# A list scheduler's model of the chip: side products kept in runs, PSUM banks counted whole, later loads

## The chip, the cores and the metric

The kernel runs on one NeuronCore of a Trainium2 chip. The metric is the device time of one execution in microseconds (us); smaller is better. TensorE is PE in the profile (its weight loads are PEld), VectorE is DVE, ScalarE is ACT, GpSimd is POOL, and SyncE is SP, which issues almost all transfers.

## What is computed

One inference step of a four-layer trunk on 384 tokens (128 context, 256 latent) of width 2048, in float32 from end to end. Each layer does

```
x += gate * W_out( mixer(RMSNorm(x) * (1 + scale) + shift) * silu(z) )
(shift, scale, gate) = silu(cond) @ W_ada_l + b_ada_l
```

Layers 0 and 3 mix by windowed attention (16 heads, 4 key heads), layer 1 by neighbourhood attention (16 heads), layer 2 by a gated MLP with normed spatial mixing. Weights of about 580 MB are read once.

## The kernel before

Every big product is made exact enough by splitting both operands into a high and a low part (`H`, `L` for a weight unit, `hH`, `hL` for the activations) and adding three fp32r products: high by high, high by low, low by high. A weight unit is 128x1024 (512 KB). SP loads it into one of four `raw` buffers, ACT copies it to `H`, DVE subtracts to get `L`, and PE multiplies: 24 products of 384 columns ("A" form: the output has 384 tokens) or 18 of 512 columns ("B" form, 3 token blocks). These are 13,824 **main products**, and all of them read `hH` or `hL`. The rest on PE are **side products**: transposes (of queries, keys and softmax rows, by `ident`), scores (`qT` against keys, and a mask added through `identR`), probabilities times values (`PTH`, `PLT`), the small condition products (`sT`, `spad`, four column tiles each), `sel`, `ones` and the mixing products of layer 2 (`aux`).

DVE also makes two thirds of the condition products by itself: it takes a transposed weight tile `araw` (512 KB, two buffers, loaded by SP) and the broadcast condition `cbc`, and reduces their product, twice for each tile (lines named `junk<-araw,cbc`). When such a pass goes from one half of the condition to the other, `cbc` is loaded again from `srow`.

The score group of one head (`head`) writes two PSUM banks, `b0` and `b1`: the context block and the first latent block go to `b0`, the second to `b1`. DVE then takes row maxima of these banks (`vmax`, in the trace `sm<-bk`).

What sets the order: the program first records all operations in the order of its Python code (class `Rec`, method `add`) and then emits them in an order of its own. `add` notes for each operation which earlier ones it needs: `data` (it waits until they are done) or `order` (same engine, it only follows). Main products are chained to each other and keep their order (`self.main`). Ranges within a tile are told apart in grains of 8 columns (`span`), so for a PSUM bank a read of the first 128 columns does not touch a write of the others. `cost` gives each operation a duration and a latency, `in_order` makes a first timetable, `due` the latest time by which each operation is wanted, and `schedule` is a list scheduler: the engine that can start first takes its ready operation with the smallest key (PE: the number in the program; others: the due time). Three passes of `due` and `schedule` follow each other (`order`). `schedule` before has a rule for PE: an operation under 100 ns (`long` is false) is held back in favour of one over 100 ns while a weight load (`LDW`, 108 ns apart, `LAG` 56 ns before the product) would not be finished. A transfer counts as landed 1300 ns after its turn in the queue.

The emitted order is fixed for each engine; the waits between engines are put in when the program is built, and those on a PSUM bank hold for the bank's users as they then stand in the order.

Of the kernel before, what the change touches and what calls it, by code (L numbers as in the profile page):

```python
# [10 lines left out]
F32R = mybir.dt.float32r  # L11
# [38 lines left out]
class Rec:  # L50
# [9 lines left out]
    def __init__(self, nc):  # L60
        self.real, self.ops, self.bytes = nc, [], {}
        for e in ("tensor", "vector", "scalar", "gpsimd", "sync"):
            setattr(self, e, _Eng(self, e))
        self.wr, self.rd, self.bank, self.tiles, self.main = {}, {}, {}, {}, None

    @staticmethod
    def span(ap):

        if not hasattr(ap, "tensor"):
            ap = ap[:, :]  # L70
        name = re.match(r"[A-Za-z]+\d*", ap.tensor.name).group()
        p = [[int(v) for v in x] for x in ap.ap]
        if name in ("i", "o"):
            return None
        if name in ("xs", "srow"):
            return name, 0, 8, name
        lo = int(ap.offset) % max(p[0][0], 1)
        hi = lo + sum(s * (n - 1) for s, n in p[1:] if s > 0) + 1
        return name, lo, hi, ap.tensor.name
# [8 lines left out]
    def cost(self, e, op, a, k):  # L88

        n = self.cols(a[0] if a else k["out"])  # L90
        if e == "tensor":
            if op == "transpose":
                d = 57
            elif "tile_position" in k:
                d = 128
            elif a[2].dtype == F32R:
                d = (n + 32) / 2.4 if n > P else 57
            else:
                d = max(4 * (n + 16) / 2.4, 224)
            return d, d + 190  # L100
        if e == "vector":
            if op == "tensor_tensor_reduce":
                return n / 0.96 + 250, n / 0.96 + 330
            if op in ("tensor_tensor", "tensor_copy", "bn_stats", "tensor_reduce"):
                m = self.cols(k.get("in_", a[1] if len(a) > 1 else None)) if op == "tensor_reduce" else 512 if op == "bn_stats" else n
                d = m / 0.96 + 72
            elif op == "scalar_tensor_tensor":
                d = n / 0.96 + (129 if hasattr(k["scalar"], "ap") else 70)
            elif op == "tensor_scalar":
                d = n / 1.92 + 190  # L110
            else:
                d = n / 0.96 + 90
            return d, d + 90
        if e == "scalar":
            if op == "dma_start":
                return 400, 2600
            d = n / 1.2 + 97 + (75 if hasattr(k.get("scale"), "ap") or hasattr(k.get("bias"), "ap") else 0)
            d += 95 if "accum_out" in k else 0
            return d, d + 115
        if e == "gpsimd":  # L120
            return 650 + 140 * n, 750 + 140 * n
        return 330, 2100
# [7 lines left out]
    def add(self, e, op, a, k):  # L130
        i = len(self.ops)
        w = [k[x] for x in self.OUTS if x in k] + ([a[0]] if a else [])
        r = [v for x, v in k.items() if x not in self.OUTS] + list(a[1:])
        w = [self.span(x) for x in w]
        r = [self.span(x) for x in r if hasattr(x, "ap") or hasattr(x, "tensor")]
        data, order = set(), set()
        G = self.GRAIN
        for s in r + w:
            if s:
                t = self.tiles.get(s[0])  # L140
                if t is None or t[0] != s[3]:
                    for x in t[1] if t else ():
                        (order if self.ops[x][0] == e else data).add(x)
                    self.tiles[s[0]] = s[3], [i]
                elif t[1][-1] != i:
                    order.add(t[1][0])
                    t[1].append(i)
        for s in r:
            if s:
                for g in range(s[1] // G, (s[2] - 1) // G + 1):  # L150
                    x = self.wr.get((s[0], g))
                    if x is not None:
                        data.add(x)
        for s in w:
            if s:
                for g in range(s[1] // G, (s[2] - 1) // G + 1):
                    x = self.wr.get((s[0], g))
                    if x is not None:
                        (order if self.ops[x][0] == e == "tensor" else data).add(x)
                    for x in self.rd.get((s[0], g), ()):  # L160
                        (order if self.ops[x][0] == e else data).add(x)
                if s[0][:2] == "bk" and e == "tensor":
                    x = self.bank.get(s[0])
                    if x is not None:
                        order.add(x)
                    self.bank[s[0]] = i
        if e == "tensor" and any(s and s[0] in ("hH", "hL") for s in r):
            if self.main is not None:
                order.add(self.main)
            self.main = i  # L170
        self.ops.append((e, op, a, k))
        for s in r:
            if s:
                for g in range(s[1] // G, (s[2] - 1) // G + 1):
                    self.rd.setdefault((s[0], g), []).append(i)
        for s in w:
            if s:
                for g in range(s[1] // G, (s[2] - 1) // G + 1):
                    self.wr[s[0], g] = i
                    self.rd[s[0], g] = []  # L180
        if not hasattr(self, "dep"):
            self.dep, self.dur, self.lat, self.eng, self.load, self.long = [], [], [], [], [], []
        order -= data
        self.dep.append([(x, True) for x in data] + [(x, False) for x in order])
        d, l = self.cost(e, op, a, k)
        self.dur.append(d)
        self.lat.append(l)
        self.eng.append("tensor vector scalar gpsimd sync".split().index(e))
        self.long.append(d > 100)
        self.load.append(self.dma_bytes(a) / 395.0 if op == "dma_start" else 0)  # L190

    SEM, LDW, LAG = 45, 108, 56

    def ready_at(self, i, start, done, margin=0):
        t, e = 0.0, self.eng[i]
# [5 lines left out]
                t = v  # L201
        return t

    def in_order(self):

        n = len(self.ops)
        free, dma = [0.0] * 5, 0.0
        start, done = [0.0] * n, [0.0] * n
        load = last = 0.0
        for i in range(n):  # L210
            e = self.eng[i]
            t = max(free[e], self.ready_at(i, start, done))
            if e == 0:
                load = max(load + self.LDW, last)
                t = last = max(t, load + self.LAG)
            start[i] = t
            free[e] = t + self.dur[i]
            if self.load[i]:
                dma = max(dma, t + 700) + self.load[i]
                done[i] = max(dma + 1300, t + self.lat[i])  # L220
            else:
                done[i] = t + self.lat[i]
        return start, done
# [13 lines left out]

    MARGIN = 250

    def schedule(self, late):  # L240
        n = len(self.ops)
        succ, left = [[] for _ in range(n)], [0] * n
        for i in range(n):
# [1 line left out]
            for x, _ in self.dep[i]:  # L245
                succ[x].append(i)
        start, done = [0.0] * n, [0.0] * n
        free, dma, load = [0.0] * 5, 0.0, 0.0
        wait, ready = [[] for _ in range(5)], [[] for _ in range(5)]
        key = [float(i) if self.eng[i] == 0 else late[i] for i in range(n)]  # L250
        for i in range(n):
            if not left[i]:
                heapq.heappush(wait[self.eng[i]], (0.0, i))
        count, last = 0, 0.0
        while count < n:
            best, be = None, None
            for e in range(5):
                if ready[e]:
                    t = free[e]
                    if e == 0 and not any(self.long[i] for _, i in ready[0]):  # L260
                        t = max(t, load + self.LDW + self.LAG)
                elif wait[e]:
                    t = max(free[e], wait[e][0][0])
                else:
# [5 lines left out]
                i = heapq.heappop(wait[e])[1]  # L270
                heapq.heappush(ready[e], (key[i], i))
            i = ready[e][0][1]
            if e == 0:
                if load + self.LDW + self.LAG > t and not self.long[i]:
                    i = min((i for _, i in ready[0] if self.long[i]), default=i)
                if i != ready[0][0][1]:
                    ready[0].remove((key[i], i))
                    heapq.heapify(ready[0])
                    heapq.heappush(ready[0], (-1.0, i))
                load = max(load + self.LDW, last)  # L280
                t = last = max(t, load + self.LAG)
            if e in (1, 2) and wait[e]:
                end, hold = t + self.dur[i], None
                for est, j in wait[e]:
# [7 lines left out]
            free[e] = t + self.dur[i]  # L292
            if self.load[i]:
                dma = max(dma, t + 700) + self.load[i]
                done[i] = max(dma + 1300, t + self.lat[i])
            else:
                done[i] = t + self.lat[i]
            count += 1
# [4 lines left out]
        return start, done  # L303

    def order(self, passes=3):
        start, done = self.in_order()
        for _ in range(passes):
            start, done = self.schedule(self.due(start))
# [1461 lines left out]
```

## Time and profile before

| what | value |
|---|---|
| three runs | 3052.76, 3053.60, 3056.09 us (median 3053.6) |
| the profiled execution | 3048.99 us, of which the span from first to last instruction is 3047.2 |
| PE busy | 3005.5 us (99%), 17,064 products |
| PE weight loads busy | 2733.9 us (90%) |
| DVE busy | 2085.1 us (68%) |
| ACT busy | 1202.4 us (39%) |
| DMA | 598.95 MB, mean 197 GB/s |
| mean granted PE clock | 0.998 |

PE's busy time counts products that overlap as one; a product is shown from its start to the end of its pipeline, so 384 columns show 0.33 us though the next one starts 0.17 us later. What a product costs is therefore read from start to start. Idle time in brackets in a timeline is the engine's, with the operation that ended it.

Stages by the trace: layer 0 to 645 us (its startup to about 180), layer 1 to 1405, layer 2 from 1405 to 2508 (its first products, for the mixing input, to about 1680), then layer 3.

### The profile page before, as it was taken

The numbers are of one execution on the slowest core, as the hardware profiler recorded it, in microseconds if no ns is written. First come the engines' busy times: TensorE is split into PE (matmuls) and PEld (weight loads), VectorE is DVE, ScalarE is ACT, GpSimd is POOL, SyncE is SP. The second block draws the span as 40 slices with busy tenths as digits, with TensorE's granted clock in tenths as the row PEclk, the third lists the DMA queues.
The fourth block names the chain that finished last, engine by engine and source line by source line (L and its number), as shares of the span: only waits on it lengthen the run. The fifth ranks groups of instructions, "written<-read, shape, count | busy, mean of one in ns | idle before, by whom it ended". The sixth has DMA issues, their size and how long they took to land.

```text
span 3047.2 us, 44052 instructions
## 1 busy us (share of the span) xinstructions
PE 3005.5 (99%) x17064; PEld 2733.9 (90%) x17064; DVE 2085.1 (68%) x3499; ACT 1202.4 (39%) x2175; POOL 59.0 (2%) x29
## 2 busy tenths in 40 slices
PE   8999999999999999999999999999999999999999
PEld 4788899988888888998878999999999998888999
DVE  4568798669898988899898974334355556444554
ACT  3344445353444444534223222222233235354542
POOL 0000000000000000000000000000000000000000
PEclk9999999999999999999999999999999999999999
DMA  9857667767676777788788663444454454333433
GB/s 384 327 164 233 206 194 250 265 212 232 210 230 211 230 214 254 249 271 275 255 261 261 200 194 123 126 126 123 128 159 138 143 188 135 121 98 104 135 108 125
DMA packets 187354, 598.95 MB, mean 197 GB/s; under 512 B 21764, under 2 KB 47620, under 8 KB 187140
## 3 DMA queue, kind: packets, MB, share of 16 engines
q1 hardware_dynamic: 186712, 596.00, 60.4%
q8 instruction: 133, 2.18, 0.3%
q14 instruction: 77, 0.63, 0.1%
q10 hardware_dynamic: 432, 0.13, 0.0%
HBM read 580.31 MB, written 15.75 MB: 196 GB/s over the span
## 4 chain that ended last, share of the span: by engine, by line
PE 87%; DVE 5%; DMA 5%; issue 2%; ACT 1%; SPq 0%; DVEq 0%; ACTq 0%
PE bk L314 87%; DMA araw<-i_w_adaT 3%; DVE junk L314 2%; DVE L L314 2%; DMA raw<-i_win_B 0%; DVE pair L314 0%; DMA cbc<-srow 0%; DVE bn L314 0%; DMA pair<-i_xT 0%; DVE sm L314 0%; ACT Pt L314 0%; DVE Pt L314 0%; ACT H L314 0%; DMA pair<-i_masks 0%; DMA sel<-i_sel 0%
## 5 line engine op out<-in xcount | busy, mean ns | idle before, releaser
L314 ACT ACTIVATE H<-raw 128x1024 fp32r<-128x1024 f32 x640 | 678.2, 1060 | 1498.8 <-PE bk L314 1378.4
L314 DVE TENSOR_TENSOR L<-raw,H 128x1024 fp32r<-128x1024 f32 x640 | 782.4, 1223 | 447.3 <-ACT H L314 445.6
L314 PE MATMUL bk<-hH,H 128*128 128x384 f32 x3072 | 1040.4, 339 | 3.6 <-DVE pair L314 3.6
L314 PE MATMUL bk<-hL,H 128*128 128x384 f32 x3072 | 1034.0, 337 | 0.0
L314 PE MATMUL bk<-hH,L 128*128 128x384 f32 x3072 | 1031.5, 336 | 0.7 <-DVE L L314 0.7
L314 PE MATMUL bk<-H,hH 128*128 128x512 f32 x1536 | 607.7, 396 | 5.7 <-ACT hH L314 3.8
L314 PE MATMUL bk<-L,hH 128*128 128x512 f32 x1536 | 605.4, 394 | 1.4 <-DVE L L314 1.2
L314 PE MATMUL bk<-H,hL 128*128 128x512 f32 x1536 | 601.9, 392 | 0.0
L314 PEld LDWEIGHTS bk<-hH,H 128*128 128x128 f32 x3072 | 578.1, 188 | 14.1 <-DVE pair L314 5.0
L314 PEld LDWEIGHTS bk<-hH,L 128*128 128x128 f32 x3072 | 577.7, 188 | 1.5 <-DVE L L314 1.0
L314 PEld LDWEIGHTS bk<-hL,H 128*128 128x128 f32 x3072 | 578.1, 188 | 1.0
L314 PEld LDWEIGHTS bk<-H,hH 128*128 128x128 f32 x1536 | 288.6, 188 | 68.9 <-issue 5.7
L314 PEld LDWEIGHTS bk<-L,hH 128*128 128x128 f32 x1536 | 288.6, 188 | 61.0 <-DVE L L314 4.4
L314 PEld LDWEIGHTS bk<-H,hL 128*128 128x128 f32 x1536 | 288.5, 188 | 58.0 <-issue 0.4
L314 DVE CUSTOM_DVE_ANT_0 junk<-araw,cbc,accA 128x1024 bf16<-128x1024 f32 x240 | 307.4, 1281 | 38.7 <-DMA araw<-i_w_adaT 19.3
L314 DVE CUSTOM_DVE_ANT_0 junk<-araw,cbc,bada 128x1024 bf16<-128x1024 f32 x240 | 307.4, 1281 | 18.8 <-DMA araw<-i_w_adaT 16.9
L314 DVE SCALAR_TENSOR_TENSOR pair<-bk,ada,pair 128x256 f32<-128x256 f32 x320 | 119.4, 413 | 213.2 <-PE bk L314 212.0
L314 ACT ACTIVATE pair<-bk 128x512 f32<-128x512 f32 (+3 forms) x162 | 89.5, 555 | 59.4 <-PE bk L314 57.8
L314 PE MATMUL bk<-pair,qT 128*128 128x384 f32 (+2 forms) x336 | 86.0, 343 | 5.2 <-DVE sm L314 4.3
L314 DVE TENSOR_TENSOR pair<-pair,aux 128x512 f32<-128x512 f32 (+1 forms) x108 | 59.8, 589 | 18.8 <-ACT pair L314 15.5
L314 ACT ACTIVATE PTH<-bk 128x512 fp32r<-128x512 f32 (+1 forms) x112 | 54.0, 514 | 40.3 <-PE bk L314 39.8
L314 ACT ACTIVATE junk<-pair 128x128 bf16<-128x128 f32 x216 | 66.5, 308 | 6.0 <-DVE accA L314 1.4
(155 smaller groups left out, 1970.6 us busy)
## 6 DMA issues: line engine op xcount, KB each, us to landing
araw<-i_w_adaT SPq DMA_DIRECT2D x240, 512.0 KB, 4.5
pair<-i_w_ada SPq DMA_DIRECT2D x96, 512.0 KB, 6.8
raw<-i_win_B SPq DMA_DIRECT2D x96, 512.0 KB, 3.7
raw<-i_nat_B SPq DMA_DIRECT2D x96, 512.0 KB, 4.3
raw<-i_win_O SPq DMA_DIRECT2D x64, 512.0 KB, 3.7
raw<-i_gm_V SPq DMA_DIRECT2D x64, 512.0 KB, 4.5
raw<-i_gm_U SPq DMA_DIRECT2D x64, 512.0 KB, 3.6
raw<-i_gm_Z SPq DMA_DIRECT2D x64, 512.0 KB, 3.6
```

Source lines behind the costliest of these rows:

```text
L314: getattr(getattr(self.real, e), op)(*a, **k)
```

## The change

Only the class `Rec` changes, that is the model that orders the operations; which operations there are, their shapes and their transfers stay as they are. Five things:

- A PSUM bank counts whole: `span` returns one range for any access to a `bk` tile, so a read of a part of a bank is taken to need every earlier write to it.
- Neighbouring transposes and fp32r side products form a chunk (`side`, `chunk`): each follows the one before, `join` gives the first of them what any of them needs, and in `schedule` the later ones get key -1, so that a chunk that has begun is finished before PE takes anything else.
- The rule for short products on PE and its weight-load clock are removed.
- Durations on PE: 84 or 109 ns for a transpose (57 before), 135 for a condition product (128), at least 112 for an fp32r product (57 before for 128 columns).
- A transfer counts as landed 1500 ns after its turn in the first timetable and 4000 ns in the passes that follow (1300 in both before).

```diff
+        if name[:2] == "bk":
+            return name, 0, 8, name
...
-                d = 57
+                d = 84 if a[0].dtype == F32R else 109
             elif "tile_position" in k:
-                d = 128
+                d = 135
             elif a[2].dtype == F32R:
-                d = (n + 32) / 2.4 if n > P else 57
+                d = max((n + 32) / 2.4, 112)
...
             self.main = i
+            self.side = None
+        elif e == "tensor" and (op == "transpose" or a[2].dtype == F32R):
+            if self.side is None:
+                self.side = i
+            elif self.side != i:
+                order.add(i - 1)
+        else:
+            self.side = None
         self.ops.append((e, op, a, k))
+        self.chunk.append(i if self.side is None else self.side)
...
+    def join(self):
+
+        for i, c in enumerate(self.chunk):
+            if c != i:
+                have = set(x for x, _ in self.dep[c])
+                self.dep[c] += [(x, d) for x, d in self.dep[i] if x < c and x not in have]
...
-    def in_order(self):
+    def in_order(self, land=1500):
...
-                done[i] = max(dma + 1300, t + self.lat[i])
+                done[i] = max(dma + land, t + self.lat[i])
...
-    def schedule(self, late):
+    def schedule(self, late, land=4000):
...
-        key = [float(i) if self.eng[i] == 0 else late[i] for i in range(n)]
+        key = [(float(i) if self.chunk[i] == i else -1.0) if self.eng[i] == 0 else late[i] for i in range(n)]
...
-            if e == 0:
-                if load + self.LDW + self.LAG > t and not self.long[i]:
-                    i = min((i for _, i in ready[0] if self.long[i]), default=i)
...
     def order(self, passes=3):
+        self.join()
```

How this moves instructions, at three places. The lines of the changed kernel are numbered four higher.

**PE, a score group of layer 0** (the one that starts at 388.93 us in the trace of before): `bk_115` is `b0`, `bk_116` is `b1`. Before:

```order
L314 MATMUL bk_115<-ck_213,qT 128x128 x2
L314 MATMUL bk_116<-pair_88_214,qT 128x384
L314 MATMUL bk_115<-ck_213,qT 128x128
L314 MATMUL bk_115<-pair_88_214,qT 128x384
L314 MATMUL bk_115<-mask,identR 128x128
L314 MATMUL bk_115<-pair_89_215,qT 128x384
L314 MATMUL bk_115<-pair_88_214,qT 128x384
L314 MATMUL bk_116<-mask,identR 128x128
L314 MATMUL bk_116<-pair_89_215,qT 128x384
L314 MATMUL bk_116<-pair_88_214,qT 128x384
```

and now:

```order
L318 MATMUL bk_115<-ck_213,qT 128x128 x3
L318 MATMUL bk_115<-pair_88_214,qT 128x384
L318 MATMUL bk_115<-mask,identR 128x128
L318 MATMUL bk_115<-pair_89_215,qT 128x384
L318 MATMUL bk_115<-pair_88_214,qT 128x384
L318 MATMUL bk_116<-pair_88_214,qT 128x384
L318 MATMUL bk_116<-mask,identR 128x128
L318 MATMUL bk_116<-pair_89_215,qT 128x384
L318 MATMUL bk_116<-pair_88_214,qT 128x384
```

The group now stands in the program's order, bank after bank. Before, the last product into `b0` waits for DVE's first maximum of the bank; now that maximum waits for the last product into `b0`, and no product of the 48 score groups waits for a maximum of its own group (18 did). Over the whole program the side products stand in 244 uninterrupted runs, 523 before.

**DVE in layer 1** (about 1206 to 1215 us in the trace of before): the condition passes on `araw`, the weight splits `L`, and the low part of a head's queries, `qT`. Before:

```order
L314 TENSOR_TENSOR L_75<-raw_70,H_72 128x1024
L314 ISA junk,accA<-araw_407_533,cbc,bada 128x1024
L314 ISA accA 128x1
L314 ISA junk,accA<-araw_408_534,cbc,bada 128x1024
L314 ISA accA 128x1
L314 TENSOR_TENSOR L_76<-raw_67,H_73 128x1024
L314 TENSOR_TENSOR qT<-bk_117,qT 128x384
L314 SCALAR_TENSOR_TENSOR pair_417_543<-pair_417_543,bk_113 128x384
```

and now:

```order
L318 TENSOR_TENSOR L_75<-raw_70,H_72 128x1024
L318 ISA junk,accA<-araw_407_533,cbc,bada 128x1024
L318 ISA accA 128x1
L318 ISA junk,accA<-araw_407_533,cbc,bada 128x1024
L318 ISA accA 128x1
L318 TENSOR_TENSOR qT<-bk_117,qT 128x384
L318 TENSOR_TENSOR L_76<-raw_67,H_73 128x1024
L318 SCALAR_TENSOR_TENSOR pair_417_543<-pair_417_543,bk_113 128x384
L318 ISA junk,accA<-araw_408_534,cbc,bada 128x1024
```

`qT` and the split now stand ahead of the first pass on tile `araw_408`, behind which they stood.

**DVE at the first mixing of layer 2** (about 1679 to 1690 us): the statistics `mv`, the scaling of the first mixing input (`pair_474`), splits and condition passes. Before:

```order
L314 BN_AGGR mv<-bn 128x2
L314 ISA junk,ada_94<-araw_552_678,cbc,accA 128x1024
L314 ISA ada_94 128x1
L314 TENSOR_TENSOR L_74<-raw_70,H_71 128x1024
L314 BN_AGGR mv<-bn 128x2
L314 ISA junk,ada_94<-araw_553_679,cbc,accA 128x1024
L314 ISA ada_94 128x1
L314 TENSOR_SCALAR st_100<-mv 128x3
L314 ISA junk,ada_94<-araw_553_679,cbc,accA 128x1024
L314 ISA ada_94 128x1
L314 TENSOR_TENSOR L_75<-raw_67,H_72 128x1024
L314 TENSOR_SCALAR pair_474_600<-pair_474_600,mv,st_101 128x512 x3
```

and now:

```order
L318 BN_AGGR mv<-bn 128x2
L318 ISA junk,accA<-araw_542_668,cbc,bada 128x1024
L318 ISA accA 128x1
L318 TENSOR_TENSOR L_74<-raw_70,H_71 128x1024
L318 BN_AGGR mv<-bn 128x2
L318 ISA junk,accA<-araw_542_668,cbc,bada 128x1024
L318 ISA accA 128x1
L318 TENSOR_SCALAR st_100<-mv 128x3
L318 TENSOR_TENSOR L_75<-raw_67,H_72 128x1024
L318 TENSOR_SCALAR pair_474_600<-pair_474_600,mv,st_101 128x512 x3
```

One condition pass less stands between the statistics and the scaling, and the passes are ten tiles behind where they were (tile 542 for 552), on the other side of the reload of `cbc`: they write `accA` still, where they wrote `ada` before.

## Rows read from the trace of the kernel before

**Rows 1.** Page, busy time by engine, share of the span, instructions:

```profile
PE 3005.5 (99%) x17064; PEld 2733.9 (90%) x17064; DVE 2085.1 (68%) x3499; ACT 1202.4 (39%) x2175; POOL 59.0 (2%) x29
```

**Rows 2.** Waits of PE, whole span: waited for, us in total, times, longest:

```profile
PE bk L314 <- DVE pair L314: 8.4, 7, 2.9
PE bk L314 <- DVE sm L314: 6.9, 18, 1.3
```

**Rows 3.** Timeline of PE, the score group at 389 us: start, length, operation:

```profile
388.76 0.33 PE L314 MATMUL bk<-hH,L 128*128 128x384 f32 x1
388.93 0.33 PE L314 MATMUL bk<-ck,qT 128*128 128x128 f32 x2
...
389.39 0.39 PE L314 MATMUL bk<-pair,qT 128*128 128x384 f32 x1
389.62 0.23 PE L314 MATMUL bk<-mask,identR 128*128 128x128 f32 x1
389.68 0.39 PE L314 MATMUL bk<-pair,qT 128*128 128x384 f32 x1
390.45 0.44 PE L314 MATMUL bk<-pair,qT 128*128 128x384 f32 x1 [0.38 <-DVE sm L314]
```

**Rows 4.** Timeline of DVE, the maximum of the same group:

```profile
390.11 0.29 DVE L314 TENSOR_REDUCE sm<-bk 128x1 f32<-128x128 f32 x1 [0.72 <-PE bk L314]
```

**Rows 5.** Timeline of PE, transposes between main products:

```profile
1233.54 0.38 PE L314 MATMUL bk<-ident,Pt 128*128 128x128 f32 x2
1233.68 0.42 PE L314 MATMUL bk<-hH,H 128*128 128x384 f32 x1
1233.94 0.38 PE L314 MATMUL bk<-ident,Pt 128*128 128x128 f32 x2
```

**Rows 6.** Timeline of PE, a run of six short products of layer 2:

```profile
1727.07 0.83 PE L314 MATMUL bk<-aux,pair 128*128 128x128 f32 x6
1727.65 0.42 PE L314 MATMUL bk<-hH,H 128*128 128x384 f32 x1
1727.91 0.34 PE L314 MATMUL bk<-hL,H 128*128 128x384 f32 x1
```

**Rows 7.** Groups of PEld: the weight loads of transposes (count, busy us, mean ns):

```profile
L314 PEld LDWEIGHTS bk<-ident,pair 128*128 128x128 f32 x216 | 29.3, 140 | 9.3 <-issue 3.5
```

**Rows 8.** Timeline of PE, the score group at 1213 us:

```profile
1214.81 0.50 PE L314 MATMUL bk<-pair,qT 128*128 128x128 f32 x2 [0.90 <-DVE qT L314]
1216.68 0.79 PE L314 MATMUL bk<-pair,qT 128*128 128x256 f32 x2 [1.25 <-DVE sm L314]
```

**Rows 9.** Timeline of DVE, the same place:

```profile
1211.86 1.28 DVE L314 CUSTOM_DVE_ANT_0 junk<-araw,cbc,bada 128x1024 bf16<-128x1024 f32 x1 [3.37 <-DMA araw<-i_w_adaT]
...
1214.21 0.55 DVE L314 TENSOR_TENSOR qT<-bk,qT 128x384 fp32r<-128x384 f32 x1
```

**Rows 10.** Busy time by stretch: PE, PEld, DVE, ACT, POOL, granted clock, DMA:

```profile
1216.20:1223.00 6.80, 6.32 (x23) 6.32 (x24) 6.21 (x15) 0.00 (x0) 0.00 (x0) 0.51 0.81 229
...
1690.80:1694.20 3.40, 3.29 (x12) 3.15 (x12) 3.40 (x6) 0.00 (x0) 0.00 (x0) 0.50 0.74 155
```

**Rows 11.** Timeline of PE, main products at the low clock:

```profile
1222.07 0.52 PE L314 MATMUL bk<-hH,H 128*128 128x384 f32 x1
1222.39 0.52 PE L314 MATMUL bk<-hL,H 128*128 128x384 f32 x1
```

**Rows 12.** Waits of DVE, then of PE, from 1440 to 1691 us:

```profile
DVE junk L314 <- DMA araw<-i_w_adaT: 14.8, 21, 1.2
DVE junk L314 <- DMA cbc<-srow: 9.2, 5, 2.9
...
PE bk L314 <- DVE pair L314: 2.9, 1, 2.9
PE bk L314 <- DVE L L314: 1.9, 4, 0.7
```

**Rows 13.** Timeline of PE at the border from layer 1 to layer 2:

```profile
1400.12 0.71 PE L314 MATMUL bk<-PH,ones 128*128 128x128 f32 x4 [1.15 <-DVE PH L314]
```

More of the change, by code (lines that the diff above doesn't have):

```diff
@@ L64, in __init__ @@
         self.wr, self.rd, self.bank, self.tiles, self.main = {}, {}, {}, {}, None
+        self.side, self.chunk = None, []
     @staticmethod
@@ L181, in add @@
         if not hasattr(self, "dep"):
-            self.dep, self.dur, self.lat, self.eng, self.load, self.long = [], [], [], [], [], []
+            self.dep, self.dur, self.lat, self.eng, self.load = [], [], [], [], []
         order -= data
@@ L188, in add @@
         self.eng.append("tensor vector scalar gpsimd sync".split().index(e))
-        self.long.append(d > 100)
         self.load.append(self.dma_bytes(a) / 395.0 if op == "dma_start" else 0)
-    SEM, LDW, LAG = 45, 108, 56
+    SEM = 45
+    def join(self):
[3 more added lines that the diff above has]
+                self.dep[c] += [(x, d) for x, d in self.dep[i] if x < c and x not in have]
     def ready_at(self, i, start, done, margin=0):
@@ L208, in in_order @@
         start, done = [0.0] * n, [0.0] * n
-        load = last = 0.0
         for i in range(n):
@@ L247, in schedule @@
         start, done = [0.0] * n, [0.0] * n
-        free, dma, load = [0.0] * 5, 0.0, 0.0
+        free, dma = [0.0] * 5, 0.0
         wait, ready = [[] for _ in range(5)], [[] for _ in range(5)]
-        key = [float(i) if self.eng[i] == 0 else late[i] for i in range(n)]
+        key = [(float(i) if self.chunk[i] == i else -1.0) if self.eng[i] == 0 else late[i] for i in range(n)]
         for i in range(n):
@@ L253, in schedule @@
                 heapq.heappush(wait[self.eng[i]], (0.0, i))
-        count, last = 0, 0.0
+        count = 0
         while count < n:
@@ L259, in schedule @@
                     t = free[e]
-                    if e == 0 and not any(self.long[i] for _, i in ready[0]):
-                        t = max(t, load + self.LDW + self.LAG)
                 elif wait[e]:
@@ L272, in schedule @@
             i = ready[e][0][1]
-            if e == 0:
-                if load + self.LDW + self.LAG > t and not self.long[i]:
-                    i = min((i for _, i in ready[0] if self.long[i]), default=i)
[L276 to L281, printed above, removed]
             if e in (1, 2) and wait[e]:
@@ L294, in schedule @@
                 dma = max(dma, t + 700) + self.load[i]
-                done[i] = max(dma + 1300, t + self.lat[i])
+                done[i] = max(dma + land, t + self.lat[i])
             else:
```

2 lines of the change are left out of this document (removed).

## The prediction

> **What bounds the kernel now.** I read the page first: PE is busy for 99% of the span and DVE for 68% [rows 1]. PE is the bound, but its busy time says little about what can be gained, since a waiting product still counts while its pipeline drains. So the next views are the waits of PE by releaser [rows 2] and the timelines around them. Main products follow each other in 0.17 us when they have 384 columns (388.76 to 388.93 in [rows 3]), and no order can make them faster. A change of order can win in three ways: PE's waits, the price of a short product by its neighbours, and stretches at the low clock.
>
> The waits that stand out are 18 for DVE's `sm`, the row maxima, 6.9 us in all [rows 2]. In one of them the product before the wait starts at 389.68 and the next, into the same bank, at 390.45 [rows 3]: 0.77 us where the same kind took 0.23 (389.39 to 389.62). Of the 0.54 us lost the profile calls 0.38 idle; the other 0.16 is restart. In that gap DVE, idle for 0.72 us until PE had written the first part, takes the maximum of 128 columns at 390.11 [rows 4], and the last product into that bank waits for it. This is not an engine that is short of time but an order in which a reader stands between two writers of one bank.
>
> The second place is layer 1 at 1214 us. PE waits 0.90 us for `qT` and 1.25 for `sm` [rows 8]. DVE was late because it had stood 3.37 us before a condition pass whose `araw` tile had not landed; `qT` stood behind that pass [rows 9]. In the 6.8 us that follow the granted clock is 0.51, the 1.2 GHz level [rows 10], and main products step at 0.32 us instead of 0.17 [rows 11].
>
> The third is the way into layer 2, 1440 to 1691 us. DVE stands 14.8 us before `araw` and 9.2 before `cbc`; PE waits 1.9 us in four waits for `L` and 2.9 in one for the first mixing input [rows 12]. After that wait, too, the clock is 0.50 for 3.4 us [rows 10].
>
> **The change part by part.** The sum is made against the profiled execution, 3048.99 us, which is 4.6 us below the median of the three runs; the same difference is then applied to the median.
>
> *Banks count whole.* The maximum of `b0` now follows the last product into `b0`, and none of the 18 waits is left in the order. Price: 6.9 us idle plus 18 restarts of 0.16 us = 2.9, so **-9.8 us**. The maxima come later by the rest of the group (0.77 us in [rows 3]); they are wanted for an exponential, transposes and values that the plan places later, and DVE is 68% busy, so I cost that at nothing. If the cover went, one head's transposes would wait 0.77 us. Bounds: 0 if the waits return elsewhere, -9.8 if none does.
>
> *Whole runs.* There are 279 fewer runs (523 to 244), so 279 times a short product now follows a short one. Interleaved, two transposes and a main product take 0.40 us (1233.54 to 1233.94 [rows 5]); less 0.17 for the main product that is 0.115 us for each transpose. In a run, six short products and the main product behind them take 0.84 us (1727.07 to 1727.91 [rows 6]), less 0.17, or 0.112 each. So a short product costs the same either way: **0**. Bounds: -0.003 x 279 = -0.8; and if the whole weight load of 0.140 us [rows 7] came out in a run, +0.025 x 279 = +7. I take the run that was seen.
>
> The Trainium skill, page "TensorE: Matmul & The Clock Gate", section "Step-by-step: what each phase is for", speaks against this: weights for the next product load while the present one runs, so a short product behind a long one should hide its load, and only in a run should loads show. By the page's formula in "Back-to-back issue gap" an interleaved product of 128 columns would take about 56 ns. By that rule the sum would be some 15 us worse; the trace's 0.115 us between long products [rows 5] does not agree.
>
> *Runs that wait for all their operands.* The first of a chunk is planned when every member's operands are ready, which guards against waits inside. But the third context score, which needs `qT`'s low part from DVE, now comes directly behind the first two; before, a product of 384 columns stood between in some groups. One of 48 groups waited for it, 0.90 us [rows 8], 1.06 with restart. I allow three: **+3.2 us**; bounds 0 and 48.
>
> *Loads land late, layer 1.* The plan's transfer was too fast: DVE met passes whose tile was not there. With 4000 ns instead of 1300 the pass on `araw_408` stands behind `qT` and the split. The 0.90 us wait with its restart goes, 1.06; and if no group waits, so should the low clock after it: 6.3 us of PE's work [rows 10] at 0.32 instead of 0.17 us a product, 6.3 x (1 - 0.17/0.32) = 2.95. Together **-4.0 us**; bounds 0 and -4.0. What is late next is the condition vector itself: passes are ten tiles behind at layer 2, 20 passes. Nothing reads them before layer 3 or the output product, hundreds of us on, and DVE is half idle then; cost nothing.
>
> *Loads land late, layer 2.* The passes at the `cbc` reload move behind the first mixing, and one pass less stands between statistics and scaling. DVE's 24.0 us before transfers [rows 12] are what made it late. If most go, PE's five waits go: 2.9 + 1.9 + 5 x 0.16 = 5.6; and the low clock: 3.4 x (1 - 0.17/0.32) = 1.6. **-7.2 us**; bounds 0 and -7.2.
>
> *Border from layer 1 to 2.* The products that spread the norm stand behind a few more condition products. PE waited 1.15 us there [rows 13], which these fill, but the first main product may wait as much longer: **0**, bounds -1.15 and +1.15.
>
> *SP* issues the same transfers; its order follows the engines that free buffers. In layer 0's startup, to 180 us, order and waits stay as they are. No pass has fewer instructions on any engine.
>
> Sum: -9.8 + 0 + 3.2 - 4.0 - 7.2 + 0 = **-17.8 us**. From 3053.6 that is **3035.8 us** (0.58% faster). A measurement of this kernel tells about 0.2%, 6.1 us, from no change.
>
> **The rivals.**
>
> *A: only the bank waits go.* The late-transfer waits move to other passes and the clock still drops. For it: the condition tiles still have two buffers, and DVE must still do all 240 tiles. Against it: the two places at which PE suffered are rearranged in the order shown. -9.8 + 3.2 = -6.6, so 3047.0; with fewer new waits 3043.8.
>
> *B: given back in the chunks.* If seven or eight groups wait 1.06 us for `qT`, the sum of A is within 2 us of nothing: 3051 to 3053. For it: [rows 8] shows the wait exists. Against it: one group of 48 had it, behind a 3.37 us stall that is the plan's error.
>
> *C: slower, by `qT` waits in most heads.* The same mechanism, at the score group's third product. It comes 0.12 us behind the first instead of up to 0.40, so DVE's subtraction must end that much earlier. At 1.06 us each, the gain of the forecast without its allowance (21.0 us) is gone at 20 groups; with 30 of 48 the kernel would take 3053.6 - 21.0 + 31.8 = 3064. Against it: DVE is not short of time outside the way into layer 2, and runs are held until all is ready in the plan.
>
> *D: interleaving did hide loads*, so that runs cost 0.054 us more at 279 joints, +15: 3051. Rows 5 and 6 together speak against it. The page named above is what speaks for it.
>
> That the change does not do what it says is excluded by the order.
>
> **How the numbers follow.** Forecast 0.58, A 0.25, B 0.08, C 0.05, D 0.04. Faster by over 0.2%: the forecast, and most of A (0.24 of 0.25): 0.82. Within: B, D and the rest of A: 0.13. Slower: C, 0.05. The range reaches from the forecast without new waits and with the small gains (-17.8 - 3.2 - 0.8 - 1.15 = -23, 3030.6; half the spread of three runs, 1.6, below that) to A: **3029 to 3047**.
>
> **What would show it right or wrong.** Right: no wait of PE for `sm` in the list of waits, against 18; in a score group, products in the bank order with no gap; transposes in runs of seven stepping at 0.11 us; DVE's waits for `araw` and `cbc` between 1440 and 1691 us well under 24.0 us; at most one stretch at the low clock besides the end. Wrong: new waits of PE for `qT` in tens; runs with steps above 0.12 us; the wait for the first mixing input still near 2.9 us. A later layer 2 or 3 that waits for the condition vector would upset the forecast altogether.

## The result and the profile after

| | kernel before | changed kernel |
|---|---|---|
| median of four runs, us | 3054.85 | 3020.78 |
| lowest and highest, us | 3052.76, 3057.01 | 3017.95, 3023.72 |
| profiled execution, us | 3048.99 | 3017.95 |

The ratio is 0.9889 with a 95% interval of 0.9871 to 0.9906: 34.1 us less, where 17.8 were forecast. The direction was right; the time lies 8 us below the lower end of the range.

The page of the changed kernel, busy time by engine, beside [rows 1]:

```profile
PE 2990.9 (99%) x17064; PEld 2731.8 (91%) x17064; DVE 2090.5 (69%) x3499; ACT 1200.4 (40%) x2175; POOL 58.6 (2%) x29
```

The same instructions, and nearly the same busy time on every engine. What changed is what PE waits for. All waits of PE in the changed kernel (waited for, us in total, times, longest), beside [rows 2]:

```profile
PE bk L318 <- DVE spad L318: 11.1, 1, 11.1
PE bk L318 <- ACT hH L318: 3.4, 4, 2.0
PE bk L318 <- DVE pair L318: 3.0, 4, 1.2
PE bk L318 <- DMA pair<-i_w_ada: 2.0, 1, 2.0
PE bk L318 <- DVE PLT L318: 1.1, 2, 0.9
PE bk L318 <- DVE Pt L318: 0.7, 1, 0.7
```

None for `sm`, none for `qT`, none for `L`. Of the 21.3 us that are left, 13.1 (`spad` and the transfer) lie before the first main product.

The score group of [rows 3] now, timeline of PE (start, length, operation):

```profile
383.25 0.45 PE L318 MATMUL bk<-ck,qT 128*128 128x128 f32 x3
383.54 0.39 PE L318 MATMUL bk<-pair,qT 128*128 128x384 f32 x1
383.76 0.22 PE L318 MATMUL bk<-mask,identR 128*128 128x128 f32 x1
383.82 0.75 PE L318 MATMUL bk<-pair,qT 128*128 128x384 f32 x3
384.40 0.22 PE L318 MATMUL bk<-mask,identR 128*128 128x128 f32 x1
384.46 0.57 PE L318 MATMUL bk<-pair,qT 128*128 128x384 f32 x2
384.88 0.34 PE L318 MATMUL bk<-hH,H 128*128 128x384 f32 x1
```

From its first product to the next main product the group takes 1.63 us (383.25 to 384.88). Before, it took from 388.93 [rows 3] to 391.20, 2.27 us, as the last row of the group there shows:

```profile
391.20 0.34 PE L314 MATMUL bk<-hH,H 128*128 128x384 f32 x1
```

So one wait for `sm` had cost 0.64 us, 0.38 of it shown as idle.

Where the 31 us between the two profiled executions went can be read from the traces, because the 13,824 main products stand in the same order in both kernels: the difference of the start of the k-th one in both traces is the gain up to there. The table takes it at nine places; the times at its left are those of before, the column "forecast" spreads the terms of the prediction over the stages, and the last four columns are experiments below (each a profiled execution against that of before).

| stage, us of before | forecast | changed | banks only | landing only | runs only | banks + landing |
|---|---|---|---|---|---|---|
| to 180 | 0 | -1.6 | 0.0 | -1.2 | +0.2 | -1.4 |
| 180 to 645, layer 0 | -1.1 | -4.5 | +2.9 | -2.0 | -1.7 | -3.2 |
| 645 to 1200, layer 1 | -3.6 | -4.6 | -3.4 | -0.1 | -1.5 | -4.7 |
| 1200 to 1235, the late `qT` | -5.4 | -5.6 | +0.2 | -5.7 | -4.3 | -5.7 |
| 1235 to 1430, border | -0.4 | -1.3 | +2.7 | -0.8 | +4.5 | -0.3 |
| 1430 to 1700, into layer 2 | -7.2 | -9.2 | -2.8 | -9.2 | -2.7 | -9.2 |
| 1700 to 2530 | 0 | -0.1 | 0.0 | 0.0 | -0.1 | 0.0 |
| 2530 to the end, layer 3 | -3.2 | -4.2 | -3.8 | 0.0 | +2.5 | -3.8 |
| waits for `qT`, placed nowhere | +3.2 | | | | | |
| sum | -17.7 | -31.0 | -4.2 | -18.9 | -3.0 | -28.2 |

(The profiled execution with banks only, 3044.76 us at a mean granted clock of 0.997, was the longest of its six, which is why that column is small.) The places that the forecast named are there, and each gave what it was priced at or a little more. What was missed is spread over places priced at nothing, and 3 us are not in any one execution (below).

DVE's waits for transfers show where to look. Kernel before, waits of DVE over the whole span:

```profile
DVE junk L314 <- DMA araw<-i_w_adaT: 36.2, 40, 3.4
DVE junk L314 <- DMA cbc<-srow: 17.4, 12, 2.9
```

The changed kernel:

```profile
DVE junk L318 <- DMA cbc<-srow: 5.6, 5, 1.6
DVE junk L318 <- DMA araw<-i_w_adaT: 2.5, 2, 1.4
```

53.6 us became 8.1. (How much of that PE feels is another matter: with 2500 ns, below, 31.1 us of it are back at the same median time.) At the place of [rows 9], timeline of DVE after:

```profile
1199.73 0.56 DVE L318 TENSOR_TENSOR qT<-bk,qT 128x384 fp32r<-128x384 f32 x1 [0.19 <-ACT qT L318]
1200.20 1.22 DVE L318 TENSOR_TENSOR L<-raw,H 128x1024 fp32r<-128x1024 f32 x1
...
1203.28 1.28 DVE L318 CUSTOM_DVE_ANT_0 junk<-araw,cbc,bada 128x1024 bf16<-128x1024 f32 x1 [1.39 <-DMA araw<-i_w_adaT]
```

DVE still meets a tile that has not landed (1.39 us), but `qT` and the split stand ahead of it now, and PE does not notice. The granted clock in the stretches that answer to [rows 10], busy time by stretch:

```profile
1204.00:1210.00 6.00, 6.00 (x38) 6.00 (x38) 5.96 (x13) 1.13 (x2) 0.00 (x0) 1.00 0.69 222
1662.00:1668.00 6.00, 6.00 (x38) 6.00 (x38) 6.00 (x10) 1.99 (x3) 0.00 (x0) 1.00 0.57 143
```

1.00 at both, the 2.4 GHz level, where before it was 0.51 and 0.50.

### The profile page after: what moved, and what is told of

Same layout as the page of the kernel before. It is cut to its first block, busy times and chain, and to the rows that moved or that the text cites. A ratio compares the mean times of both kernels' runs of the same rounds, so it can differ in the third digit from the quotient of the medians.

```text
span 3016.2 us, 43990 instructions
## 1 busy us (share of the span) xinstructions
PE 2990.9 (99%) x17064; PEld 2731.8 (91%) x17064; DVE 2090.5 (69%) x3499; ACT 1200.4 (40%) x2175; POOL 58.6 (2%) x29
## 4 chain that ended last, share of the span: by engine, by line
PE 98%; DVE 1%; DMA 0%; ACT 0%; issue 0%; SPq 0%; DVEq 0%; ACTq 0%
PE bk L318 98%; DMA pair<-i_xT 0%; DVE pair L318 0%; DMA sel<-i_sel 0%; DVE PLT L318 0%; DVE Pt L318 0%; DVE junk L318 0%; ACT Pt L318 0%; DVE L L318 0%; ACT H L318 0%; ACT PLT L318 0%; ACT PTH L318 0%; ACT hH L318 0%; ACT junk L318 0%; ACT pair L318 0%
## 5 line engine op out<-in xcount | busy, mean ns | idle before, releaser
L318 PE MATMUL bk<-L,hH 128*128 128x512 f32 x1536 | 599.0, 390 | 0.1
L318 PE MATMUL bk<-pair,qT 128*128 128x384 f32 (+2 forms) x336 | 74.1, 329 | 0.0
```

Of the source, the lines that this page charges most:

```text
L318: getattr(getattr(self.real, e), op)(*a, **k)
```

## The experiments

Theory 1 was formed from the table's third column: the gains add up, about 10 us from the banks, about 20 from the landing times all over the kernel, nothing from the runs. The rivals: whole runs carry the unforeseen 13 us (34.1 less the 21.0 that the forecast had without its allowance for `qT`); or late landing is worth only the two places of the forecast.

### One part of the change alone

**Banks whole, alone**, in the kernel before:

```diff
+        if name[:2] == "bk":
+            return name, 0, 8, name
```

> Only 'banks count whole' is put into the kernel before. Theory 1 (the parts add up: bank waits, late loads, and nothing from the runs): 18 waits of PE for sm go, 0.54 to 0.64 us each, so -10 us against the kernel before, about 3044; DVE still stands before araw and cbc on the way into layer 2, and the low clock after the first mixing input stays. Theory 2 (most of the unforeseen gain comes from the banks, because a head that is finished earlier or later moves everything behind it): -20 us or more, about 3034.

Measured: 3042.22 us against 3052.24, -10.0; ratio 0.9957 (0.9943 to 0.9971). Waits of PE, of which three answer to what was expected:

```profile
PE bk L316 <- DVE pair L316: 8.9, 8, 2.3
PE bk L316 <- DVE qT L316: 2.4, 1, 2.4
PE bk L316 <- DVE L L316: 1.6, 4, 0.5
```

`sm` is gone, and the waits that late transfers cause are all still there, one of them for `qT` larger than before. The six executions lie between 3031.8 and 3044.8 us, so the median is a rough one. On top of late landing, where executions scatter less, whole banks are worth 8.0 us (3030.05 to 3022.04, the experiment without runs below). Priced at -9.8, the term holds. The Trainium skill, page "PSUM — Partial Sum Buffer", section "PSUM bank collisions raise a hardware error", has a rule that would give such waits: PSUM is to be guarded by semaphores per bank (and quadrant), not by address. The trace agrees in so far as a reader of 128 columns held up a writer of others [rows 3, 4]; the price was 0.64 us each time in layer 3 (six waits, 3.8 us).

**Landing times, alone**:

```diff
-                done[i] = max(dma + 1300, t + self.lat[i])
+                done[i] = max(dma + 1500, t + self.lat[i])
...
-                done[i] = max(dma + 1300, t + self.lat[i])
+                done[i] = max(dma + 4000, t + self.lat[i])
```

> Only the landing times are changed in the kernel before (1500 ns in the first timetable, 4000 ns in the passes). Theory 1: the 18 sm waits stay, the waits behind late transfers go all over the kernel, with the low clock at both places: -20 us against the kernel before, about 3034. Rival (late loads are worth only the two places named in the forecast, 4.0 and 7.2): -11, about 3043.

Measured: 3030.05 us, -22.2; ratio 0.9925 (0.9913 to 0.9937). Waits of PE, and then of DVE for the condition transfers:

```profile
PE bk L314 <- DVE sm L314: 6.2, 18, 0.4
```

```profile
DVE junk L314 <- DMA araw<-i_w_adaT: 2.5, 2, 1.7
DVE junk L314 <- DMA cbc<-srow: 1.7, 1, 1.7
```

Bank waits are 18 again, though some are at other heads: the one of 1.25 us at 1216 us [rows 8] is gone, and three new ones stand in layer 0. DVE's 53.6 us of waits are down to 4.2. The rival, two places and no more, would have been 11. This is the largest part of the change, and the forecast had half of it. Three us of the 22 do not show in the profiled executions (-18.9): the five executions of this kernel took 3029.4 to 3030.1 us at a mean granted clock of 1.000, the 17 of the kernel before that ran beside them 3048.1 to 3057.9 at 0.995 to 0.999, and the profiled one (3048.99, 0.998) is among the shorter. So the kernel before seems to lose a different amount to the low clock in each execution, and its two stretches at the low clock in the profiled one each stand behind a wait for late loads [rows 8, 10, 12].

**Runs, alone** (chunks, `join`, the durations on PE, no rule for short products; the changed kernel without the bank lines and with 1300 ns):

```diff
-        if name[:2] == "bk":
-            return name, 0, 8, name
...
-    def in_order(self, land=1500):
+    def in_order(self, land=1300):
...
-    def schedule(self, late, land=4000):
+    def schedule(self, late, land=1300):
```

> Only the chunks, the new durations on PE and the dropped rule for short products; banks as before, landing 1300 ns as before. Theory 1: a short product costs 0.11 us in a run as between long ones, so within 0.2% of the kernel before, 3048 to 3060, with 240 runs for 523. Rival (whole runs are what the forecast undervalued): -13, about 3041. Rival on the other side (weight loads come out in runs): +7 to +15, 3061 to 3069.

Measured: 3048.56 us, -3.7; ratio 0.9990 (0.9981 to 0.9998), 0.1% and about what can be told from nothing. Neither rival came. In the changed kernel a run of transposes, timeline of PE:

```profile
1217.17 0.92 PE L318 MATMUL bk<-ident,Pt 128*128 128x128 f32 x7
1217.93 0.49 PE L318 MATMUL bk<-ident,pair 128*128 128x128 f32 x3
1218.18 0.42 PE L318 MATMUL bk<-hH,H 128*128 128x384 f32 x1
1218.44 0.34 PE L318 MATMUL bk<-hL,H 128*128 128x384 f32 x1
```

Seven transposes take 0.76 us (1217.17 to 1217.93), 0.109 each. With the three that follow, and the main product behind them, it is 1.27 us to 1218.44; less 0.17 that is 0.110 for each of ten, where a transpose between main products took 0.115 [rows 5]. In these rows the price hardly depends on the neighbours. Chunks, durations and the dropped rule were put in together; whether one of them gains what another loses is not shown.

**Banks and landing, without runs**: both diffs above in the kernel before.

> Banks count whole and late landing, without chunks, new durations or the dropped rule: side products stand between main products as before, some 520 runs. Theory 1: the whole gain, 3018 to 3026, equal to the changed kernel. Rival (whole runs carry 13 us of it): about 3034. If the banks and the landing times only help together, the sum of the runs with one of them alone falls short of this one.

Measured: 3022.04 us, -30.2; ratio 0.9899 (0.9886 to 0.9912). The sum of the two alone is -32.2. With some 520 runs where the changed kernel has 244, the time is the same.

**The changed kernel again**, on one chip with the next three.

> The changed kernel again, beside the kernel before on the same chip. Theory 1 (banks -10, late landing -22, runs -4 or nothing): 3018 to 3022, that is 0 to 4 us below the kernel with banks and late landing alone (3022.0). Rival (the runs do nothing once loads are planned late): equal to it within 1 us.

Measured: 3022.09 us beside 3052.78, ratio 0.9898 (0.9884 to 0.9912). The rival was right: on top of whole banks and late landing the runs do nothing that shows (3022.09 and 3022.04).

**The changed kernel with 1300 ns** in both places:

```diff
-    def in_order(self, land=1500):
+    def in_order(self, land=1300):
...
-    def schedule(self, late, land=4000):
+    def schedule(self, late, land=1300):
```

> The changed kernel with transfers counted as landed after 1300 ns again; banks whole and runs kept. Theory 1 (late landing is worth 22 us by itself, mostly waits of DVE for araw and cbc and the low clock that follows): 3038 to 3043, DVE's waits for araw and cbc back near 50 us. Rival (once runs wait for all their operands, late loads matter less): under 3034.

Measured: 3042.50 us, ratio 0.9967 (0.9954 to 0.9979). 20.4 us come back by this number alone, and DVE's waits with it (30.8 us for `araw`, 17.1 for `cbc`).

### Which transfers are late

In `schedule` of the kernel before, 4000 ns for one kind of tile (`nm` is the destination's name):

```diff
-                done[i] = max(dma + 1300, t + self.lat[i])
...
+                land = 4000 if nm.startswith("araw") else 1300
+                done[i] = max(dma + land, t + self.lat[i])
```

> The kernel before, with 4000 ns for transfers into araw alone; all others 1300 ns. Theory 1 (the condition tiles are what is late): DVE's 36 us of waits for araw nearly go and most of the 22 us with them, 3032 to 3040. Rival (the reload of cbc, which is what made the first mixing input late, carries it): within 8 us of the kernel before.

Measured: 3037.01 us, -15.8; ratio 0.9944 (0.9930 to 0.9958).

The same for the reload of the condition vector:

```diff
-                done[i] = max(dma + 1300, t + self.lat[i])
...
+                land = 4000 if nm.startswith("cbc") else 1300
+                done[i] = max(dma + land, t + self.lat[i])
```

> The kernel before, with 4000 ns for the reload of cbc alone. Theory 1: the wait of 2.9 us for the first mixing input and the low clock behind it go, the rest stays: -5 to -10 us, 3042 to 3047. Rival (araw alone matters): within 3 us of the kernel before.

Measured: 3040.16 us, -12.6; ratio 0.9959 (0.9946 to 0.9971), more than expected. And for all other transfers:

```diff
-                done[i] = max(dma + 1300, t + self.lat[i])
...
+                land = 4000 if not nm.startswith(("araw", "cbc")) else 1300
+                done[i] = max(dma + land, t + self.lat[i])
```

> The kernel before, with 4000 ns for all transfers except those into araw and cbc, which stay at 1300 ns. Theory 1 (only the condition tiles and the condition vector are late; weights into raw are loaded far ahead): within 3 us of the kernel before. Rival (late landing also moves weight loads): -5 us or more.

Measured: 3047.13 us beside 3051.94, -4.8; ratio 0.9979 (0.9970 to 0.9988). The time lies between theory 1 (within 3 us) and the rival (5 or more). The trace decides for the rival: weights were late too, in layer 0, where the main products gain 3.6 us. Timelines of the kernel before, ACT, DVE and PE at one place there:

```profile
236.31 1.06 ACT L314 ACTIVATE H<-raw 128x1024 fp32r<-128x1024 f32 x1 [5.88 <-DMA raw<-i_win_B]
```

```profile
237.41 1.23 DVE L314 TENSOR_TENSOR L<-raw,H 128x1024 fp32r<-128x1024 f32 x1 [2.04 <-ACT H L314]
238.55 0.55 DVE L314 SCALAR_TENSOR_TENSOR pair<-pair,bk 128x384 f32<-128x384 f32 x1
```

```profile
239.15 0.50 PE L314 MATMUL bk<-H,hH 128*128 128x512 f32 x1 [1.51 <-DVE pair L314]
```

ACT waits 5.88 us for a weight; DVE's split waits for ACT; the accumulation into `pair` stands behind the split, and PE waits 1.51 us for the bank that it empties. It is the same pattern as [rows 9], three engines long; the list of PE's waits names `pair` and not the weight, and the forecast went by that list. By the list of its waits ACT stands 30.9 us before weights from 180 to 360 us in the kernel before, 5.4 in this experiment.

The three parts sum to -33.2 where all together give -22.2: `araw` alone and `cbc` alone each remove nearly all that is lost on the way into layer 2 (9.2 and 8.7 us from 1430 to 1700 us by the main products' starts, of 9.2 with all transfers late), which can go only once.

### How late is late enough

The changed kernel with another time in the passes, first

```diff
-    def schedule(self, late, land=4000):
+    def schedule(self, late, land=2500):
```

> The changed kernel with 2500 ns for 4000 in the passes. Theory 1 (what matters is that the plan's time is not below what the trace shows behind a buffer's release): if 2500 is enough the time stays at 3020 to 3023; if the real delay is nearer to 4000, DVE's waits for araw return and it takes 3030 or more.

Measured: 3022.06 us, ratio 0.9897 (0.9882 to 0.9912). By the median 2500 ns does all that 4000 does, and yet DVE stands 17.6 us before `araw` and 13.5 before `cbc` in it, nearly four times what it does in the changed kernel. The second half of the expectation, that DVE's waits and the time go together, was wrong: most of the waits that are left do not reach PE. Not all of them: at the place of [rows 9] a wait of DVE is back, and behind it PE waits 1.40 us for `qT`.

```profile
1201.81 1.28 DVE L318 CUSTOM_DVE_ANT_0 junk<-araw,cbc,bada 128x1024 bf16<-128x1024 f32 x1 [3.70 <-DMA araw<-i_w_adaT]
```

Its profiled execution (3022.91 us, the longest of the four) gained 26.1 us by the last main product where the changed kernel gained 31.0 and, measured again, 29.7. So 2500 ns is near the edge. Then

```diff
-    def schedule(self, late, land=4000):
+    def schedule(self, late, land=8000):
```

> The changed kernel with 8000 ns for 4000. Theory 1 (a plan that takes loads for later than they are only puts condition passes further back, until the products that need the condition vector wait for them): with two araw buffers the plan can do one tile in some 4 us more, 240 tiles, so DVE's passes fall behind by hundreds of us and PE waits at a layer's start: 3060 or more. Rival (later is only safer): 3018 to 3024.

Measured: 3129.34 us, 77 more than before; ratio 1.0249 (1.0235 to 1.0263). DVE hardly waits for a transfer (4.6 us for `araw`), and PE waits for DVE and ACT. PE's waits in that kernel at the three longest places, its timeline:

```profile
1274.00 3.74 PE L318 MATMUL bk<-ident,pair 128*128 128x128 f32 x12 [19.35 <-DVE pair L318]
...
1314.81 1.00 PE L318 MATMUL bk<-ident,pair 128*128 128x128 f32 x3 [12.70 <-DVE pair L318]
...
1493.91 0.80 PE L318 MATMUL bk<-H,hH 128*128 128x512 f32 x1 [18.28 <-ACT hH L318]
```

and busy time by stretch around the first two (PE is the second figure, the granted clock the third from the end):

```profile
1260.00:1310.00 50.00, 22.69 (x108) 20.82 (x108) 34.81 (x64) 14.80 (x52) 3.21 (x1) 0.67 0.49 159
1310.00:1360.00 50.00, 33.08 (x141) 28.07 (x145) 32.80 (x80) 15.99 (x44) 3.28 (x1) 0.57 0.35 111
```

The loss is not where a layer begins alone, as expected, but also in the heads of layer 1; the lower clock after each wait adds to it. From 1430 us of before to the end it loses 1.1 us against the changed kernel.

### A run that may beat both

A run of condition products costs more than its products. Timeline of PE in the changed kernel, a run of eight and one of sixteen, each with the main product before it and the two behind it:

```profile
217.67 0.34 PE L318 MATMUL bk<-hH,L 128*128 128x384 f32 x1
217.94 0.61 PE L318 MATMUL bk<-raw,sT 128*2 128x256 f32 x8
218.48 0.44 PE L318 MATMUL bk<-hH,H 128*128 128x384 f32 x1
218.76 0.33 PE L318 MATMUL bk<-hL,H 128*128 128x384 f32 x1
```

```profile
102.60 0.40 PE L318 MATMUL bk<-H,hL 128*128 128x512 f32 x1
102.93 1.04 PE L318 MATMUL bk<-pair,sT 128*2 128x256 f32 x16
103.90 0.44 PE L318 MATMUL bk<-hH,H 128*128 128x384 f32 x1
104.18 0.33 PE L318 MATMUL bk<-hL,H 128*128 128x384 f32 x1
```

Eight: 1.09 us from 217.67 to 218.76, less two main products of 0.173, is 0.74. Sixteen: 1.58, less 0.227 and 0.173, is 1.18. So 0.055 for each product and some 0.3 for each run. Pairing the tiles that the stream brings one by one in layer 0 makes 16 such runs 8:

```diff
-R_AT = (1, 3, 5, 6, 8, 9, 11, 12)
+R_AT = (3, 3, 6, 6, 9, 9, 12, 12)
```

> The changed kernel with the 16 runs of eight small condition products on raw tiles made 8 runs of sixteen (two tiles follow each other in the stream). Theory (each run of condition products costs 0.31 us besides 0.054 for each product: 8 take 0.75 us and 16 take 1.18 in the trace): 8 fewer runs, -2.5 us, about 3019.6. Rival (two raw buffers taken at once make a weight unit late): 3024 or more.

Measured: 3014.82 us (3013.67 to 3015.19), ratio to the kernel before 0.9874 (0.9860 to 0.9887): below both kernels. That is 7.3 us below the changed kernel's second measurement, on another chip, and the two intervals overlap; on the same chip the changed kernel with 2500 ns took 3022.06. Profiled against profiled (3014.55 and 3017.95) it is 3.4: 4.1 gained from 180 to 645 us, where the pairs are, and 0.6 at the borders behind layers 1 and 2, less 0.8 by a later start and 0.5 by a later end. The trace has nine runs of condition products fewer in that stage (15 for 24), 2.7 us at 0.3 each; what the other 1.4 are is not shown. Nor is it shown that it beats the changed kernel itself by more than 4 us. The Trainium skill, page "TensorEngine Tiling (Array Packing)", section "Key Properties", says that changing the tiling mode drains TensorE. A fixed price for each run agrees with that, but that the drain is its cause is not shown, and the page gives no figure for it.

## Why the prediction was wrong

**What bounds the kernel.** Right: PE, by its waits, the clock and the price of short products, and the first two made the gain. One view of the page spoke of the rest and was not weighed, the chain of work that ended last, by engine, in the kernel before and in the changed one:

```profile
PE 87%; DVE 5%; DMA 5%; issue 2%; ACT 1%; SPq 0%; DVEq 0%; ACTq 0%
```

```profile
PE 98%; DVE 1%; DMA 0%; ACT 0%; issue 0%; SPq 0%; DVEq 0%; ACTq 0%
```

Transfers are 143 us of the chain of before. Of these 93 lie between 1405 and 1700 us, 5 at [rows 9] and 13 in the startup, which the forecast had or left alone. The other 33 are six transfers at places that it priced at nothing. Three of them lie in layer 0, each ahead of a wait of PE (start, length):

```profile
229.82 6.41 DMA raw<-i_win_B
...
312.12 5.72 DMA raw<-i_win_B
...
636.42 5.11 DMA pair<-i_masks
```

**Banks**, -9.8: -10.0 alone, -8.0 on top of late landing. Right. By the main products' starts a wait cost 0.64 us in most of layer 3 and 0.47 to 0.49 in most of layer 1, for 0.54 forecast; the one at 1216 us, 1.4 in the forecast, goes with late landing alone (-5.7 at that place) and not with whole banks alone (+0.2). No wait of PE names a maximum any more. Those for `PLT` and `Pt` grew from 0.6 to 1.8 us together; whether the later maxima have a part in that is not shown.

**Whole runs**, 0: -3.7 alone with an interval that nearly reaches none, 0 on top of the other two. Right, and rival D falls: 0.109 us in a run, 0.115 between long products. The Trainium skill, page "TensorE: Matmul & The Clock Gate", section "Back-to-back issue gap", gives about 56 ns by its formula for an isolated product of 128 columns and adds that this counts too little at such a size, against 81 ns measured. The trace agrees with neither figure.

**Runs that wait for all operands**, +3.2: not one of the 48 groups waited for `qT` in the changed kernel. The allowance was a guess from one wait that late loads had caused, and these were cured by the same change; with 1300 ns the wait for `qT` is there (2.8 us, once), and with 2500 ns too (1.4 us, once). Rivals B and C fall with it.

**Loads land late, layer 1**, -4.0 and 1.4 for the `sm` wait there: -5.6. Right.

**Loads land late, layer 2**, -7.2: -9.2. Right in kind. By the main products' starts the four waits for `L` gave 2.5, as priced; the wait for the mixing input gave 4.1, since its six products ran at the low clock too (2.00 us in the row of before below, 0.83 in a later run of six [rows 6]); the other 2.6 are put down to the low clock behind it and small gaps ahead of it.

```profile
1690.35 2.00 PE L314 MATMUL bk<-aux,pair 128*128 128x128 f32 x6 [2.86 <-DVE pair L314]
```

**Border and "SP and startup unchanged"**, 0: -1.3 and -1.6. Of the 1.6, 0.6 lies before the first main product and cannot be told from chance; the other 1.0 is a wait of PE for `pair` at 153 us (0.96), which is gone in the changed kernel and in both experiments with 4000 ns for all transfers. The order in the startup did not stay as it was.

**Layer 0**, -1.1 (two bank waits): -4.5. This is the step that failed: "loads land late" was priced at the two places that PE's longest waits had led to, and at nothing elsewhere. Of the 8.4 us that PE waited for `pair` [rows 2] the forecast priced 2.9. In layer 0 PE's waits of 1.51 us for `pair`, 0.78 for `qT` and 1.70 for `hH` (at 239, 321 and 643 us) stand behind two late weights and a late mask by way of ACT, or of ACT and DVE, as the chain above shows. With late landing alone the main products gain 4.6 us there up to 390 us and 0.7 at the last of the three; 3.3 are lost again in between, where new waits for `sm`, `PLT` and `pair` stand.

**From the profiled execution to the median**: "the same difference is then applied". It was not the same: 31.0 between the profiled executions, 34.1 between the medians, and the profiled execution of before was the shorter one for its kernel: it lies 5.9 us below the median of its four, that of the changed kernel 2.8. That the low clock, which the kernel before meets more often, makes the difference is likely and not shown.

The sum of the misses: 3.2 (`qT`) + 3.4 (layer 0) + 1.6 (to 180 us) + 2.0 (layer 2) + 0.9 (border) + 2.1 (layers 1 and 3, and the place at 1214) + 3.1 (executions) = 16.3 us, the whole difference, as it must be, since the stages cover the span. The mechanism was right. The term that was mis-sized is the landing time: -22.2 alone, and -20.2 on top of whole banks (3042.22 to 3022.04), for the -11.2 forecast. Of the 11.0 that it was short by, alone, the traces show 3.7 at the two places of the forecast (1.4 of it the bank wait at 1216 us), 4.0 at places priced at nothing (startup 1.2, layer 0 2.0, border 0.8), and 3.3 lie between executions. The second miss is the allowance of 3.2 for `qT`, which nothing in the changed kernel answers to. The range failed with the first: its lower end took in only the bounds of the terms that had been named, so the price of a cause that acts at more places was bounded by those at which it had been seen.

## What to carry to other kernels

A scheduler's model that takes transfers for faster than they are can put a wait anywhere ahead of the bound engine, not only where that engine's list of waits carries a transfer's name. Look for the places in the chain of work and in the waits of the engines that feed the bound one (here 53.6 us on DVE, and 30.9 on ACT from 180 to 360 us). Their sum is not the price: together they were worth some 22 us, layer 3 gained nothing from the landing times, and with 2500 ns 31.1 us of DVE's waits cost nothing that the median shows. So follow each one to the bound engine. A plan that is somewhat late costs nothing here (2500 and 4000 ns gave the same median), one that is far too late does (8000: 3129 us). And where waits end in a lower clock, compare medians of several executions: here they differ by 34.1 us and the two profiled ones by 31.0.

## What was not expected of the hardware

The time of one kernel goes with its mean granted clock from one execution to the next: with whole banks alone, 3031.82 us at 1.000, 3038.34 at 0.999, 3040.64 at 0.998 and 3043.80 to 3044.76 at 0.997, on one chip; with late landing alone, five executions at 1.000 within 0.7 us. The changed kernel still spreads over 5.8 us, from 3017.95 and 3018.97 at 1.000 to 3023.72 at 0.998. And a run of condition products, which use a part of the array, has a fixed price of 0.3 us on PE beside 0.055 us for each product, which no wait and no busy time on the page shows.
